# Spreading the rows of 8x8 blocks: two float32r products of 296 columns in place of one fp32 product of 392

## The chip, the cores and the metric

The kernel runs on one core of a Trainium2 chip. The metric is device microseconds of one execution; the number compared is the median of several runs. TensorE is called PE below (PEld is its weight load), VectorE DVE, ScalarE ACT, GpSimd POOL.

## The reference, cut to what matters

One decoder block on 512 tokens of width 1024: a stick-breaking attention branch and an RWKV-7 branch side by side, gated and merged, then an MLP and a gated embedding. The change lies in the RWKV-7 branch, whose recurrence is

```
state = state * w_t + (state a_t) b_t^T + v_t k_t^T
y     = state r_t
```

over 8 heads of 64 by 64. The kernel does it in chunks of 64 tokens. For each chunk and head, it needs the inverse of a unit triangular 64x64 matrix (one plus a strictly triangular matrix made of a and b). That inverse is built from the small blocks up: 8x8 blocks on the diagonal by substitution, then 32x32, then 64x64.

## The kernel before

After the attention (to about 140 us) comes the stage that holds the change, to about 400 us. It has one round for each of the four pairs of heads (pairs 0 to 3 here). A round has three kinds of work, which a scheduler puts in one fixed order on each engine:

- the fill: large products of the projections, `mm3`, three float32r matmuls of 512 columns for each step (L191, L192, L193, into `ps_m`; below "main matmuls"), with a cast of their weights on ACT (L175) and its remainder on DVE (L176), and the evacuations `u` (L304) and `gg` (L678) with `mix` (L306);
- `prepare` of the next pair: it makes the inputs of the recurrence. Two groups of products of `Q` and `BK` (L787) give the matrices, which DVE masks into `LM` (L792) and `DE` (L795). Then the inverse follows: DVE cuts out the 8x8 blocks (`own8`, L828), transposes `LM` in four quarters (L838), and adds the blocks' rows up to `L8` (L831). Then L833 puts `L8` times a selection of rows into `Ls`, a product with a block matrix of ones (L840) spreads every row over the 8 partitions of its block, and seven steps of DVE substitution (L849, L850) read it from PSUM. L851 expands the result into `own8`, and three products `times` (L817) and two more steps (L876, L884) go on to 32 and 64;
- `scan` of the pair before: 8 chunks one after the other, each with a product of the state on PE (L935), a sum on DVE (`UV`, L937), a second product (L944), and two updates of the state on DVE (`S`, L952).

PE and DVE take their instructions in the scheduler's order, so a wait of PE for one of the small results holds the fill behind it. `Ls` lies before the change in a buffer of the pool `tmp`, whose five buffers many other steps share.

The lines of the inverse that the change replaces:

```
Ls = tmp()[:, 0:392].rearrange("p (s k i) -> p s k i", s=7, k=8)
dve.tensor_tensor(out=Ls, in0=L8[..., 1:8] (7 times), in1=s8[..., 0:7], op=ALU.mult)
ps = ps_gen()[:, 0:392]
product_ = pe.matmul(ps, cc(K_BO8, P), Ls, start=True, stop=True)
```

Of the kernel before, what the change touches and what calls it, by code (L numbers as in the profile page):

```python
# [11 lines left out]
F32R = mybir.dt.float32r  # L12
BF16 = mybir.dt.bfloat16
AF = mybir.ActivationFunctionType
ALU = mybir.AluOpType
# [3 lines left out]
P = 128  # L19
# [31 lines left out]
K_ID, K_ONE, K_STRICT, K_INCL, K_B8, K_O8, K_S8, K_BO8, K_BO, K_TRI, K_NEG, K_CAUS = range(12)  # L51
# [34 lines left out]
def tile_block(ctx: ExitStack, tc: tile.TileContext, xT, xt, pT, wts, lora, cols_d, gfin_d, consts_d, out, dbg=None):  # L86
    nc = tc.nc
    act, dve, pool, pe, sync = nc.scalar, nc.vector, nc.gpsimd, nc.tensor, nc.sync
# [3 lines left out]
    def r32(ap):  # L92
        return ap.bitcast(F32)
# [20 lines left out]
    def cc(k, w):  # L114
        return cst[:, COFF[k]:COFF[k] + w]
# [161 lines left out]
    with ExitStack() as sA:  # L277
# [43 lines left out]
        with ExitStack() as s1:  # L321
# [12 lines left out]
            ps = ps_z()  # L334
# [242 lines left out]
        with ExitStack() as s2:  # L577
            p2 = s2.enter_context(tc.tile_pool(name="p2", bufs=1))
# [17 lines left out]
            pool.memset(Z, 0.0)  # L596

            NBIG, NMID = 9, 3

            def ps_gen():  # L600
                return ps2.tile([P, T], F32, name="ps_g", bufs=3)
# [13 lines left out]
            for hp in range(HP):  # L615
                csl = slice(hp * P, (hp + 1) * P)
                for i, (name, got) in enumerate((("w0", cum_), ("a0", a_all))):
                    ps = ps_gen()
                    pe.matmul(ps, lw[:, i, csl], lx[:, i], start=True, stop=False)
                    pe.matmul(ps, lw[:, i, csl], lxl[i], start=False, stop=True)  # L620
                    t = p2.tile([P, T], F32, name=name, bufs=HP)
# [9 lines left out]
            def tmp(dt=F32):  # L631
                return p2.tile([P, T], dt, name="tmp", bufs=5)
# [53 lines left out]
            def prepare(hp, got):  # L686
# [18 lines left out]
                ps = yield from head_sums(sq)  # L705
# [37 lines left out]
                ps = yield from head_sums(ke)  # L743
# [6 lines left out]
                for g in range(2):  # L750
                    ps = ps_gen()
                    for c in range(4):
                        pe.transpose(out=ps[:, c * P:(c + 1) * P],
                                     in_=BK[:, g * 4 + c, :, :].rearrange("p s t -> p (s t)"), identity=ident)
# [3 lines left out]
                ps = ps_gen()  # L758
# [8 lines left out]
                ps = ps_gen()  # L767
# [9 lines left out]
                for g in range(2):  # L777
# [11 lines left out]
                    for hh in range(2):  # L789
# [3 lines left out]
                                          in1=strict.rearrange("p (o u t) -> p o u t", o=1, u=1).broadcast_to([P, 2, 2, C]),  # L793
                                          op=ALU.mult)
                        dve.tensor_tensor(out=DE[:, hh, g * 4:g * 4 + 4, :].rearrange("p (cp q) t -> p cp q t", q=2),  # L795
                                          in0=ps4[:, :, 0::3, :],
                                          in1=incl.rearrange("p (o u t) -> p o u t", o=1, u=1).broadcast_to([P, 2, 2, C]),
                                          op=ALU.mult)
# [8 lines left out]
                s8 = cc(K_S8, 8)  # L807
# [18 lines left out]
                for r, rows in enumerate(QUADS):  # L826
# [2 lines left out]

                L8, Xt = X8[:, 0], X8[:, 1]  # L830
                dve.tensor_reduce(out=L8, in_=own8.rearrange("p k (b i) -> p k i b", b=4), axis=mybir.AxisListType.X, op=ALU.add)  # L831
                Ls = tmp()[:, 0:392].rearrange("p (s k i) -> p s k i", s=7, k=8)
                dve.tensor_tensor(out=Ls, in0=L8.rearrange("p (o k) i -> p o k i", o=1)[:, :, :, 1:8].broadcast_to([P, 7, 8, 7]),  # L833
                                  in1=s8[:, 0:7].rearrange("p (s o u) -> p s o u", o=1, u=1).broadcast_to([P, 7, 8, 7]), op=ALU.mult)
                yield
                dve.tensor_copy(out=Xt, in_=s8.rearrange("p (o i) -> p o i", o=1).broadcast_to([P, 8, 8]))
                for r, rows in enumerate(QUADS):
                    beside = dve.transpose(out=N[rows], in_=LM[rows, :, r // 2, r % 2 * 32:r % 2 * 32 + 32])  # L838
                ps = ps_gen()[:, 0:392]
                product_ = pe.matmul(ps, cc(K_BO8, P), Ls.rearrange("p s k i -> p (s k i)"), start=True, stop=True)  # L840

                tc.add_manual_dep(product_.ins, beside.ins.name,
                                  mybir.DependencyInfo(mybir.DependencyClass.NoSync, mybir.DependencyReason.DATA), reason="order")
                ps = ps.rearrange("p (s k i) -> p s k i", s=7, k=8)
                dve.tensor_tensor(out=N, in0=N, in1=o8.broadcast_to([P, 8, 32]), op=ALU.mult)
                for i in range(7):
                    n = 7 - i
                    t = own8[:, :, 0:n]
                    dve.tensor_tensor(out=t, in0=ps[:, i, :, i:7], in1=Xt[:, :, i:i + 1].broadcast_to([P, 8, n]), op=ALU.mult)  # L849
                    dve.tensor_tensor(out=Xt[:, :, i + 1:8], in0=Xt[:, :, i + 1:8], in1=t, op=ALU.add)  # L850
                dve.tensor_tensor(out=own8.rearrange("p k (b i) -> p k b i", b=4),  # L851
                                  in0=Xt.rearrange("p k (o i) -> p k o i", o=1).broadcast_to([P, 8, 4, 8]),
# [19 lines left out]
                ps = ps_gen()  # L872
# [553 lines left out]
```

## Time and profile before

| what | us |
|---|---|
| median of 3 runs | 869.69 (869.67 to 869.99) |
| the profiled execution | 869.75 |
| its span | 867.7 |
| PE busy in the span | 851.4 |
| DVE busy in the span | 678.1 |

The profile comes from one execution. Its time is 2.05 us over its span, and 0.06 us over the median. The profile writes an fp32 matmul as two records and a float32r one as one. The durations of matmuls overlap, so the time that PE gives to one is read from start to start, not from its duration.

### The profile page before, as it was taken

The page shows a single profiled execution, that of the slowest core. Times are in us where ns is not written, and L with a number is a line of the kernel's source. Part 1 is how long each engine was busy: PE and PEld are TensorE (multiplying, and loading weights), DVE is VectorE, ACT ScalarE, POOL GpSimd, SP SyncE. Part 2 cuts the span into 40 slices and gives each one's busy share as a digit, 9 for nine tenths or more (in the row PEclk, how much of TensorE's full clock was granted, in tenths as well). Part 3 has the DMA queues.
Part 4 walks back from the last instruction along what each step waited for, and adds up shares of the span by engine and source line. Part 5 has one row for each costly group of instructions (what it writes and reads, how often), then busy time and mean ns, then how long its engine had stood idle before and what let it go on. Part 6 is the DMA issues. An engine that isn't in the chain of part 4 may idle for free.

```text
span 867.7 us, 13424 instructions
## 1 busy us (share of the span) xinstructions
PE 851.4 (98%) x5182; PEld 686.8 (79%) x5182; DVE 678.1 (78%) x1228; ACT 448.6 (52%) x703; POOL 80.4 (9%) x138
## 2 busy tenths in 40 slices
PE   8999999999999999999999999999999999999996
PEld 5778787877777777777888888888888888888885
DVE  7899987896979888776754789858985987697767
ACT  6888887744335343534424464344434543453744
POOL 1432431002302111020000000000000000000000
PEclk9999999999999999999999999999999999999999
DMA  7212212221121224437935621531252034300422
GB/s 269 98 49 66 82 62 85 74 97 51 62 87 57 80 73 153 141 116 258 318 121 181 232 73 38 182 120 49 83 184 98 25 127 164 98 1 0 170 73 98
DMA packets 32272, 95.32 MB, mean 110 GB/s; under 512 B 3664, under 2 KB 3664, under 8 KB 32208
## 3 DMA queue, kind: packets, MB, share of 16 engines
q1 hardware_dynamic: 32208, 94.46, 32.6%
q8 instruction: 41, 0.67, 0.3%
q14 instruction: 23, 0.19, 0.1%
HBM read 83.96 MB, written 10.49 MB: 109 GB/s over the span
## 4 chain that ended last, share of the span: by engine, by line
PE 81%; DVE 10%; ACT 4%; issue 1%; DMA 1%; SPq 0%; POOL 0%; POOLq 0%; DVEq 0%; ACTq 0%
PE ps_m L191 13%; PE ps_m L193 13%; PE ps_m L192 13%; PE ps_m L206 9%; PE ps_m L207 9%; PE ps_m L208 9%; DVE w_lo L176 2%; PE ps_g L817 1%; PE ps_o L497 1%; PE ps_g L193 1%; PE ps_c L935 1%; PE ps_s L944 1%; PE ps_g L191 1%; PE ps_g L192 1%; PE ps_g L906 1%
## 5 line engine op out<-in xcount | busy, mean ns | idle before, releaser
L175 ACT CAST w_hi<-w_raw 128x1024 fp32r<-128x1024 f32 x94 | 99.0, 1053 | 170.4 <-PE ps_m L192 110.8
L176 DVE TENSOR_TENSOR w_lo<-w_raw,w_hi 128x1024 fp32r<-128x1024 f32 x94 | 115.1, 1225 | 37.6 <-ACT w_hi L175 37.2
L191 PE MATMUL ps_m<-h_hi,w_hi 128*128 128x512 f32 x320 | 130.6, 410 | 0.9 <-ACT h_hi L353 0.9
L192 PE MATMUL ps_m<-h_lo,w_hi 128*128 128x512 f32 x320 | 128.0, 400 | 0.0
L193 PE MATMUL ps_m<-h_hi,w_lo 128*128 128x512 f32 x320 | 127.5, 399 | 0.0
L191 PE MATMUL ps_m<-hx,w_hi 128*128 128x512 f32 x256 | 99.6, 390 | 0.4 <-ACT hx L1049 0.4
L192 PE MATMUL ps_m<-hx,w_hi 128*128 128x512 f32 x256 | 99.6, 390 | 0.0
L193 PE MATMUL ps_m<-hx,w_lo 128*128 128x512 f32 x256 | 99.5, 389 | 0.0
L191 PEld LDWEIGHTS ps_m<-h_hi,w_hi 128*128 128x128 f32 x320 | 60.7, 190 | 11.4 <-ACT h_hi L353 1.6
L193 PEld LDWEIGHTS ps_m<-h_hi,w_lo 128*128 128x128 f32 x320 | 60.3, 188 | 11.8
L192 PEld LDWEIGHTS ps_m<-h_lo,w_hi 128*128 128x128 f32 x320 | 60.5, 189 | 11.0 <-DVE h_lo L354 1.1
L191 PEld LDWEIGHTS ps_m<-hx,w_hi 128*128 128x128 f32 x256 | 48.0, 188 | 10.5 <-ACT hx L1049 0.6
L192 PEld LDWEIGHTS ps_m<-hx,w_hi 128*128 128x128 f32 x256 | 48.1, 188 | 10.2 <-DVE hx L1050 0.2
L193 PEld LDWEIGHTS ps_m<-hx,w_lo 128*128 128x128 f32 x256 | 48.0, 188 | 10.0
L207 PE MATMUL ps_m<-w_lo,fS 128*128 128x512 f32 x128 | 49.8, 389 | 0.0
L208 PE MATMUL ps_m<-w_hi,fS 128*128 128x512 f32 x128 | 49.8, 389 | 0.0
L206 PE MATMUL ps_m<-w_hi,fS 128*128 128x512 f32 x128 | 49.8, 389 | 0.0
L1291 POOL TENSOR_SCALAR r<-s 128x1 f32<-128x1 f32 x1 | 0.5, 519 | 478.9 <-DVE t L1271 478.9
L208 PE MATMUL ps_m<-w_hi,fA 128*128 128x512 f32 x96 | 37.4, 389 | 0.0
L207 PE MATMUL ps_m<-w_lo,fA 128*128 128x512 f32 x96 | 37.3, 389 | 0.0
L206 PE MATMUL ps_m<-w_hi,fA 128*128 128x512 f32 x96 | 37.3, 389 | 0.0
L221 ACT CAST fS<-sums 128x256 fp32r<-128x256 f32 (+1 forms) x32 | 19.8, 620 | 33.3 <-DVE sums L1141 33.3
(378 smaller groups left out, 1911.6 us busy)
## 6 DMA issues: line engine op xcount, KB each, us to landing
w_raw<-in_wts_dram SPq DMA_DIRECT2D x98, 512.0 KB, 3.5
gates<-gg SPq DMA_DIRECT2D x16, 256.0 KB, 2.1
x_in<-in_xT_dram SPq DMA_DIRECT2D x8, 256.0 KB, 5.7
tmp<-gates SPq DMA_DIRECT2D x8, 256.0 KB, 4.0
upsb<-tmp SPq DMA_DIRECT2D x8, 256.0 KB, 3.5
ga<-upsb SPq DMA_DIRECT2D x8, 256.0 KB, 5.4
gb<-gates SPq DMA_DIRECT2D x8, 256.0 KB, 5.4
xs<-in_xt_dram SPq DMA_DIRECT2D x4, 512.0 KB, 5.9
```

Of the source, the lines that this page charges most:

```text
L175: act.copy(out=hi, in_=raw)
L176: dve.tensor_tensor(out=lo, in0=raw, in1=r32(hi), op=ALU.subtract)
L191: pe.matmul(ps, wh, xh[:, k, t], start=first, stop=False)
L192: pe.matmul(ps, wh, xl[:, k, t], start=False, stop=False)
L193: pe.matmul(ps, wl, xh[:, k, t], start=False, stop=last)
L206: pe.matmul(ps, xh[:, k + j], wh, start=first and j == 0, stop=False, skip_group_check=True)
L207: pe.matmul(ps, xh[:, k + j], wl, start=False, stop=False, skip_group_check=True)
L208: pe.matmul(ps, xl[:, k + j], wh, start=False, stop=last and j == 1, skip_group_check=True)
L221: act.copy(out=hi, in_=src)
L497: pe.matmul(ps_o[:, j * P:T], vv[:, j, hh, :, :].rearrange("p a d -> p (a d)"), part[:, ZB[j]:ZB[j] + ZN[j]], start=j == 2 and part is wh, ...
L817: last = pe.matmul(ps[rows, k], left[rows, k, :], rhs[rows, k], start=True, stop=True)
L906: pe.matmul(ps[:, j * P:(j + 1) * P], Z[:, hh * 4 + g * 2 + cp, :], MA[:, g * 4 + j, :], start=True, stop=True)
```

## The change

`L8` is split by DVE into a float32r part and the remainder, both in a new tile `L8p`. `Ls` becomes a tile of its own with two halves of 296 columns, one for each part. A half leaves out elements that the substitution does not read: rows 0 to 2 keep 7 columns for each of 8 blocks (168 columns), rows 3 to 6 keep 4 (128 columns). Each half is thus made by two DVE multiplications. The product becomes two float32r matmuls, one after the other into the same PSUM tile, with the ones matrix as a float32r copy `bo8` that one more DVE cast makes at the start of the stage. The substitution reads its rows at other places in PSUM; its shapes stay.

```
+            bo8 = p2.tile([P, P], F32R, name="bo8")
+            dve.tensor_copy(out=bo8, in_=cc(K_BO8, P))
+            SPREAD = ((0, 3, 0), (3, 4, 168))
...
-                Ls = tmp()[:, 0:392].rearrange("p (s k i) -> p s k i", s=7, k=8)
-                dve.tensor_tensor(out=Ls, in0=L8.rearrange("p (o k) i -> p o k i", o=1)[:, :, :, 1:8].broadcast_to([P, 7, 8, 7]),
+                L8p = p2.tile([P, 2, 8, 8], F32R, name="L8p")
+                dve.tensor_copy(out=L8p[:, 0], in_=L8)
+                dve.tensor_tensor(out=L8p[:, 1], in0=L8, in1=r32(L8p[:, 0]), op=ALU.subtract)
+                Ls = p2.tile([P, 2, 296], F32R, name="Ls")
+                for u, (s0, n, at) in [(u, x) for u in range(2) for x in SPREAD]:
+                    w = 7 - s0
+                    dve.tensor_tensor(out=Ls[:, u, at:at + n * 8 * w].rearrange("p (s k i) -> p s k i", s=n, k=8),
...
-                ps = ps_gen()[:, 0:392]
-                product_ = pe.matmul(ps, cc(K_BO8, P), Ls.rearrange("p s k i -> p (s k i)"), start=True, stop=True)
+                ps = ps_gen()[:, 0:296]
+                product_ = pe.matmul(ps, bo8, Ls[:, 0], start=True, stop=False)
+                pe.matmul(ps, bo8, Ls[:, 1], start=False, stop=True)
```

The scheduler orders all of the stage anew. On DVE, pair 0, from the sum of the rows (`X` here is the tile of `L8`) to the first evacuation behind the product, the order was:

```order
L831 TENSOR_REDUCE X_1843<-own_1842 128x64
L838 STREAM_TRANSPOSE LX<-LM 32x8x32
L833 TENSOR_TENSOR tmp<-X_1843,cst 128x392
L838 STREAM_TRANSPOSE LX<-LM 32x8x32 x2
L678 TENSOR_TENSOR gg<-ps_m,rs 128x512
```

It is now, in the same place:

```order
L835 TENSOR_REDUCE X_1845<-own_1844 128x64
L850 STREAM_TRANSPOSE LX<-LM 32x8x32
L838 CAST L8p<-X_1845 128x64
L850 STREAM_TRANSPOSE LX<-LM 32x8x32
L839 TENSOR_TENSOR L8p<-X_1845,L8p 128x64
L843 TENSOR_TENSOR Ls<-L8p,cst 128x168
L843 TENSOR_TENSOR Ls<-L8p,cst 128x128
L843 TENSOR_TENSOR Ls<-L8p,cst 128x168
L843 TENSOR_TENSOR Ls<-L8p,cst 128x128
L850 STREAM_TRANSPOSE LX<-LM 32x8x32
L682 TENSOR_TENSOR gg<-ps_m,rs 128x512
```

Six instructions stand where one stood, and one of the two transpositions behind it has moved ahead of them. The rows are the same in the other pairs.

On PE, pair 3, around the product (`ps_s` and `ps_c` are the two products of the scan), the order was:

```order
L192 MATMUL ps_m<-h_lo,w_hi 128x512
L840 MATMUL ps_g<-tmp,cst 128x392
L944 MATMUL ps_s<-UV,BKt 128x128
L193 MATMUL ps_m<-h_hi,w_lo 128x512
L191 MATMUL ps_m<-h_hi,w_hi 128x512
L192 MATMUL ps_m<-h_lo,w_hi 128x512
L193 MATMUL ps_m<-h_hi,w_lo 128x512
L191 MATMUL ps_m<-h_hi,w_hi 128x512
L192 MATMUL ps_m<-h_lo,w_hi 128x512
L193 MATMUL ps_m<-h_hi,w_lo 128x512
L935 MATMUL ps_c<-S_1570,Q 128x128
```

It is now:

```order
L192 MATMUL ps_m<-h_lo,w_hi 128x512
L852 MATMUL ps_g<-Ls,bo_1582 128x296
L853 MATMUL ps_g<-Ls,bo_1582 128x296
L193 MATMUL ps_m<-h_hi,w_lo 128x512
L958 MATMUL ps_s<-UV,BKt 128x128
L191 MATMUL ps_m<-h_hi,w_hi 128x512
L192 MATMUL ps_m<-h_lo,w_hi 128x512
L193 MATMUL ps_m<-h_hi,w_lo 128x512
L949 MATMUL ps_c<-S_1570,Q 128x128
L191 MATMUL ps_m<-h_hi,w_hi 128x512
L192 MATMUL ps_m<-h_lo,w_hi 128x512
L958 MATMUL ps_s<-UV,BKt 128x128
```

The scan's steps stand closer together behind the product: 1, 3 and 2 main matmuls lie between them in place of 0, 7 and 6.

The main matmuls between the last L787 and the product number 23, 24, 21 and 20 in pairs 0 to 3 before, and 25, 24, 26 and 24 after. In pairs 1 and 3 the new order has among them the two scan steps that pair 2 had before (`ps_s`, 9 main matmuls, `ps_c`); in pair 2 it has the one that pair 1 had (`ps_c`, then all main matmuls). The two matmuls of the product have a wait each, the first for the first half of `Ls`, the second for the second. Between the product and the first `times` there are 25, 38, 35 and 43 main matmuls before, and 38, 40, 38 and 40 after.

## Rows read from the trace of the kernel before

**Rows 1.** The page: busy time of the engines, and the chain that ended last by engine.

```profile
PE 851.4 (98%) x5182; PEld 686.8 (79%) x5182; DVE 678.1 (78%) x1228; ACT 448.6 (52%) x703; POOL 80.4 (9%) x138
...
PE 81%; DVE 10%; ACT 4%; issue 1%; DMA 1%; SPq 0%; POOL 0%; POOLq 0%; DVEq 0%; ACTq 0%
```

**Rows 2.** Busy time by stretch: the stretch, its length, then PE, PEld, DVE, ACT and POOL busy with counts, the granted clock of PE, DMA share and GB/s.

```profile
260.00:300.00 40.00, 39.44 (x353) 30.35 (x351) 35.42 (x87) 16.97 (x26) 8.45 (x14) 1.00 0.22 73
```

**Rows 3.** The timeline of PE around the product of pair 0: start, duration, engine, instruction, and in brackets the idle time before it and what ended it.

```profile
186.38 0.39 PE L193 MATMUL ps_m<-h_hi,w_lo 128*128 128x512 f32 x1
...
186.60 0.39 PE L191 MATMUL ps_m<-h_hi,w_hi 128*128 128x512 f32 x1
...
187.12 0.30 PEld L840 LDWEIGHTS ps_g<-tmp,cst 128*128 128x128 f32 x2 [0.55 <-DVE tmp L833]
187.12 0.93 PE L840 MATMUL ps_g<-tmp,cst 128*128 128x392 f32 x2
...
187.58 0.69 PE L192 MATMUL ps_m<-h_lo,w_hi 128*128 128x512 f32 x1
...
188.11 0.39 PE L193 MATMUL ps_m<-h_hi,w_lo 128*128 128x512 f32 x1
```

**Rows 4.** The same for pairs 1, 2 and 3: the main matmul ahead of the product, and the product.

```profile
233.49 0.39 PE L192 MATMUL ps_m<-h_lo,w_hi 128*128 128x512 f32 x1
...
234.44 0.93 PE L840 MATMUL ps_g<-tmp,cst 128*128 128x392 f32 x2 [0.56 <-DVE tmp L833]
...
286.10 0.39 PE L192 MATMUL ps_m<-h_lo,w_hi 128*128 128x512 f32 x1
...
286.66 0.93 PE L840 MATMUL ps_g<-tmp,cst 128*128 128x392 f32 x2 [0.17 <-DVE tmp L833]
...
337.42 0.39 PE L192 MATMUL ps_m<-h_lo,w_hi 128*128 128x512 f32 x1
...
337.78 0.93 PE L840 MATMUL ps_g<-tmp,cst 128*128 128x392 f32 x2
```

**Rows 5.** The timeline of PE in the attention: float32r matmuls of 256 and of 384 columns that follow each other.

```profile
81.22 0.28 PE L497 MATMUL ps_o<-wh,vv 128*128 128x256 f32 x1
81.33 0.28 PE L497 MATMUL ps_o<-wl,vv 128*128 128x256 f32 x1
...
81.92 0.33 PE L509 MATMUL ps_z<-sums_hi,neg 128*128 128x384 f32 x1
82.09 0.34 PE L509 MATMUL ps_z<-sums_lo,neg 128*128 128x384 f32 x1
```

**Rows 6.** The timeline of DVE ahead of the product of pair 0.

```profile
182.69 0.41 DVE L792 TENSOR_TENSOR LM<-ps_g,cst 128x256 f32<-128x256 f32 x1
...
183.02 0.41 DVE L795 TENSOR_TENSOR DE<-ps_g,cst 128x256 f32<-128x256 f32 x1
...
185.44 0.56 DVE L831 TENSOR_REDUCE X<-own 128x64 f32<-128x256 f32 x1
...
186.03 0.43 DVE L838 STREAM_TRANSPOSE LX<-LM 32x256 f32<-32x256 f32 x1
...
186.50 0.57 DVE L833 TENSOR_TENSOR tmp<-X,cst 128x392 f32<-128x392 f32 x1
...
187.10 0.89 DVE L838 STREAM_TRANSPOSE LX<-LM 32x256 f32<-32x256 f32 x2
```

**Rows 7.** Groups of DVE instructions by line and shape: count, busy us and mean ns of one, and the idle time before them with what ended it.

```profile
L536 DVE CAST bones<-first 128x128 fp32r<-128x128 f32 x1 | 0.2, 219 | 0.0
...
L836 DVE COPY X<-cst 128x64 f32<-128x64 f32 x4 | 0.7, 163 | 3.1 <-DMA o_sb<-oo 3.1
...
L478 DVE TENSOR_TENSOR sums<-sp,sums 128x128 f32<-128x128 f32 x8 | 2.4, 294 | 0.0
...
L849 DVE TENSOR_TENSOR own<-ps_g,X 128x56 f32<-128x56 f32 x4 | 0.8, 203 | 0.0
```

**Rows 8.** The timeline of pair 2, between its two groups of L787: the second group on PE, and `UV` and the first mask of the second group on DVE.

```profile
279.89 1.13 PE L787 MATMUL ps_g<-Q,BK 64*128 64x128 f32 x14
...
280.43 0.29 DVE L937 TENSOR_TENSOR UV<-ps_c,UV 64x128 f32<-64x128 f32 x1
280.86 0.42 DVE L792 TENSOR_TENSOR LM<-ps_g,cst 128x256 f32<-128x256 f32 x1
```

**Rows 9.** The waits of PE in the stage: PE instruction, what it waited for, us in total, times, longest.

```profile
PE ps_s L944 <- DVE UV L937: 0.9, 3, 0.3
```

**Rows 10.** The timeline of PE at `times`: the first product of pair 0, the first of pair 3, the third of pair 3, and L884 in pair 0.

```profile
194.19 0.74 PE L817 MATMUL ps_g<-LX,own 32*32 32x32 f32 x64 [0.45 <-DVE own L851]
...
203.52 0.58 PEld L884 LDWEIGHTS ps_g<-Z,LX 32*32 32x32 f32 x32 [0.37 <-issue]
...
350.13 0.64 PEld L817 LDWEIGHTS ps_g<-LX,own 32*32 32x32 f32 x64 [0.47 <-DVE own L851]
...
355.08 0.64 PEld L817 LDWEIGHTS ps_g<-LX,LB 32*32 32x32 f32 x64 [1.15 <-DVE LX L863]
```

**Rows 11.** The timeline of DVE in pair 1: from the start of an evacuation, over a weight's remainder and the end of a mix with two steps of the substitution between them, to the start of L851.

```profile
242.44 0.67 DVE L304 TENSOR_TENSOR u<-ps_m,rs 128x512 f32<-128x512 f32 x1
...
244.99 0.41 DVE L851 TENSOR_TENSOR own<-X,cst 128x256 f32<-128x256 f32 x1
```

More of the change, by code (lines that the diff above doesn't have):

```diff
@@ L831, in prepare @@
                 dve.tensor_reduce(out=L8, in_=own8.rearrange("p k (b i) -> p k i b", b=4), axis=mybir.AxisListType.X, op=ALU.add)
-                Ls = tmp()[:, 0:392].rearrange("p (s k i) -> p s k i", s=7, k=8)
-                dve.tensor_tensor(out=Ls, in0=L8.rearrange("p (o k) i -> p o k i", o=1)[:, :, :, 1:8].broadcast_to([P, 7, 8, 7]),
-                                  in1=s8[:, 0:7].rearrange("p (s o u) -> p s o u", o=1, u=1).broadcast_to([P, 7, 8, 7]), op=ALU.mult)
+                L8p = p2.tile([P, 2, 8, 8], F32R, name="L8p")
[5 more added lines that the diff above has]
+                    dve.tensor_tensor(out=Ls[:, u, at:at + n * 8 * w].rearrange("p (s k i) -> p s k i", s=n, k=8),
+                                      in0=r32(L8p[:, u:u + 1, :, 1 + s0:8]).broadcast_to([P, n, 8, w]),
+                                      in1=s8[:, s0:s0 + n].rearrange("p (s o u) -> p s o u", o=1, u=1).broadcast_to([P, n, 8, w]),
+                                      op=ALU.mult)
                 yield
@@ L838, in prepare @@
                     beside = dve.transpose(out=N[rows], in_=LM[rows, :, r // 2, r % 2 * 32:r % 2 * 32 + 32])
-                ps = ps_gen()[:, 0:392]
-                product_ = pe.matmul(ps, cc(K_BO8, P), Ls.rearrange("p s k i -> p (s k i)"), start=True, stop=True)
+                ps = ps_gen()[:, 0:296]
+                product_ = pe.matmul(ps, bo8, Ls[:, 0], start=True, stop=False)
+                pe.matmul(ps, bo8, Ls[:, 1], start=False, stop=True)
                 tc.add_manual_dep(product_.ins, beside.ins.name,
                                   mybir.DependencyInfo(mybir.DependencyClass.NoSync, mybir.DependencyReason.DATA), reason="order")
-                ps = ps.rearrange("p (s k i) -> p s k i", s=7, k=8)
+                rows_ = [ps[:, at:at + n * 8 * (7 - s0)].rearrange("p (s k i) -> p s k i", s=n, k=8)[:, j, :, j:7 - s0]
+                         for s0, n, at in SPREAD for j in range(n)]
                 dve.tensor_tensor(out=N, in0=N, in1=o8.broadcast_to([P, 8, 32]), op=ALU.mult)
@@ L848, in prepare @@
                     t = own8[:, :, 0:n]
-                    dve.tensor_tensor(out=t, in0=ps[:, i, :, i:7], in1=Xt[:, :, i:i + 1].broadcast_to([P, 8, n]), op=ALU.mult)
+                    dve.tensor_tensor(out=t, in0=rows_[i], in1=Xt[:, :, i:i + 1].broadcast_to([P, 8, n]), op=ALU.mult)
                     dve.tensor_tensor(out=Xt[:, :, i + 1:8], in0=Xt[:, :, i + 1:8], in1=t, op=ALU.add)
```

## Prediction

> **What bounds the kernel now.** I read the page first. PE is busy for 851.4 of 867.7 us and carries 81% of the chain that ended last; DVE carries 10% of it [rows 1]. Then I read the busy time by stretch: in the rounds of the stage PE is busy for 39.44 of 40 us at the full granted clock, and DVE for 35.42 [rows 2]. So PE is the bound, and what it does is worth its full price; but DVE is close behind it, and each result of DVE that comes late holds the whole queue of PE. Last I read the timelines of both engines around the product, where the change lies. A main matmul takes 0.23 us from start to start. Ahead of the product of pair 0, PE could have gone on at 186.60 + 0.23 = 186.83, and the product starts at 187.12, when `Ls` is there: a wait of 0.29 us [rows 3]. By the same reading pairs 1, 2 and 3 wait for 0.72, 0.33 and 0.13 us [rows 4]. PE already waits for `Ls` in all four pairs, 1.47 us in sum. That decides how the change is to be costed: whatever DVE takes longer for `Ls` goes to the path, unless the new order of PE has more work ahead of the product.
>
> **The product itself.** From its start at 187.12 to where the next main matmul would have started by the pace of those behind it (188.11 - 0.23 = 187.88), the fp32 product takes 0.76 us of PE [rows 3]. Float32r matmuls that follow each other take 0.11 us for 256 columns and 0.17 us for 384 [rows 5], so 296 take 0.13, and two take 0.27 (bounds 0.22 and 0.34). PE gains 0.49 us for each pair, **1.96 us** in all (1.7 to 2.2).
>
> **When Ls is ready.** Before, the second transposition starts at 186.03, L833 at 186.50, and `Ls` is there at 187.07 [rows 6]. Now, from 186.50: the cast of 64 elements (0.16, as the copy of 64), a transposition (0.43 and 0.04 of change-over on either side), the remainder (0.20, as the 56 elements of L849), then the four multiplications [rows 6, 7]. A multiplication of 128 elements takes 0.29, one of 168 lies between that and 0.41 for 256; I take 0.33 [rows 6, 7]. DVE instructions that don't need each other start 0.08 before the end of the one ahead: 0.41 long, 0.33 from start to start [rows 6]. That gives the cast to 186.66, the transposition to 187.12, the remainder to 187.36, the first half of `Ls` to 187.83 and the second to 188.29. The first half is **0.76 us later**, the second **1.22**. At full length plus 0.03 of change-over each it would be 0.97 and 1.65. One transposition (0.44) less stands behind them.
>
> **What PE does meanwhile.** Pair 0 has 2 main matmuls more ahead of the product: the wait for the first half is 0.29 + 0.76 - 0.46 = 0.59. The second matmul then waits for 1.22 - 0.76 - 0.13 = 0.33 in every pair: 0.92 in sum. Pair 2 now has the order of pair 1 before, with 2 more: 0.72 + 0.76 - 0.46 + 0.33 = 1.35. Pairs 1 and 3 have that of pair 2 before, with 3 more: 0.33 + 0.76 - 0.69 + 0.33 = 0.73. In pair 1 DVE has besides the remainder of a head sum (0.60) between the two groups of masks, and PE reaches the second group 2 main matmuls (0.46) sooner. DVE was only 0.14 early there, from the end of `UV` at 280.72 to 280.86 [rows 8], so 0.60 + 0.46 - 0.14, about 0.9, come on top: 1.63. Pair 3 has one main matmul less there, 0.1: 0.83. The four waits make 0.92 + 1.63 + 1.35 + 0.83 = 4.73 us, against 1.47 now: **+3.26 us**. So the product's own gain is more than taken back at its own place.
>
> **What stands behind it.** L944 now waits for `UV` three times, 0.31 each [rows 9], since the two transpositions stand ahead of `UV`. With one transposition behind `Ls`, and 2, 2 and 1 main matmuls between, I get 0.15, 0.15 and 0.37: **-0.3**. At the first `times`, pair 0 now waits 0.45 for `own8` [rows 10]. DVE gets an evacuation, a weight's remainder and a mix ahead of it (2.55 us less 0.15 for the small steps between, so 2.4 [rows 11]) and loses 0.44; PE gets 13 main matmuls (2.96) and loses 0.63 of the product. The wait goes: **-0.4**. In pair 3 PE has 3 main matmuls less (0.69) and 0.63 less of the product, DVE 0.44 less: a wait of 0.12 (0.47 less the 0.35 or so that stands ahead of such products with no wait at all, as at L884 [rows 10]) becomes 1.0: **+0.9**, in part already at the scan's steps, which stand closer there. The third `times` of pair 3 waits 1.15 - 0.35 = 0.8 [rows 10] and gets 2 main matmuls more ahead of it: **-0.45**. Pairs 1 and 2 come out even. The cast of `bo8` (0.22 [rows 7]) stands where the copy into `X` now waits 3.1 us for a store [rows 7]; it takes over that wait, and the evacuation behind it on DVE is only 0.1 later. I cost it at nothing, since PE has its fill there; it costs 0.2 if that cover is gone. `Ls` leaves the pool `tmp`, which could end a wait of a later `tmp`: 0 to -0.3, taken as nothing.
>
> **The sum.** -1.96 + 3.26 - 0.3 - 0.4 + 0.9 - 0.45 = +1.05 us on the profiled 869.75, which lies 0.06 over the median: **870.7 us**, no change that a measurement of this kernel can tell, for it tells about 0.2% or 1.74 us (867.95 to 871.43). The terms that I read from other pairs in place of the pair itself (the waits of pairs 1 to 3, and those at `times`) are each good to some 0.5 us; together that is about 1.2 us either way.
>
> **The rivals.** *The waits do not grow* (faster). The scheduler has moved main matmuls ahead of the product in pairs 0, 2 and 3 and the first `times` of pair 0 further back. If DVE reaches the masks earlier than in the pairs that I took as patterns, by 0.7 us or more in each pair, the waits stay at their 1.5 us and only the product's gain is left: 869.7 - 1.96 = 867.7. For it speaks that DVE is not full (35.42 of 40), against it that all four pairs wait now. It decides for faster from 2.8 us less wait than I have. *The short DVE instructions do not overlap* (slower). The second half of `Ls` and the remainder hang on results of just before, and the row that shows 0.33 from start to start is of instructions that do not. At full length plus 0.03 of change-over, the second half comes after 1.65 and not 1.22, 0.43 later in each pair, 1.7 us in all: 872.4. The point from which it makes the kernel measurably slower is 0.7 us, that is 0.18 in each pair, or 0.30 from one multiplication to the next and not 0.25. [...] *The product is not cheaper* (slower): if the float32r product took what the fp32 one takes, the time would be 870.7 + 1.96 = 872.7. The rows of the attention speak against it [rows 5].
>
> **How the numbers follow.** My forecast, within 0.2%, gets 0.53. The waits that do not grow, faster by over 0.2%, get 0.15. Slower by over 0.2% gets 0.32: 0.27 for the short instructions (with the errors of the patterns to that side), 0.05 for the product. The range goes from 867.8 to 872.8. Below it I leave out about half of the first rival, above it half of the last and the far part of the second, in sum 0.18.
>
> **What would show it.** Two matmuls of L852 and L853 with 0.13 us of PE each, and ahead of each a wait for `Ls`, 0.4 to 1.3 us for the first and about 0.3 for the second. DVE rows of 0.16, 0.20, 0.33 and 0.29 us, with 0.25 from one multiplication to the next. A PE busy time some 2 us down with the span up, or level. A first `times` with no wait in pair 0, and one of about 1 us in pair 3. The prediction is wrong if the first matmul finds its half ready, or if PE's waits in the stage outside these places change by more than 1 us, for the whole stage was ordered anew and I followed only the places around the product.

## The result, and the profile after

| | median us | runs | lowest to highest |
|---|---|---|---|
| before | 869.43 | 12 | 868.60 to 870.18 |
| after | 871.83 | 12 | 870.59 to 877.53 |

The changed kernel takes 1.0041 times as long (95% interval 1.0024 to 1.0057): 2.4 us more, slower by more than the 0.2% that a measurement can tell. The profiled execution of it took 871.73 us, 1.98 more than that of the kernel before.

The page of the changed kernel, busy times and the chain that ended last:

```profile
PE 851.4 (98%) x5182; PEld 686.1 (79%) x5182; DVE 682.3 (78%) x1249; ACT 448.8 (52%) x703; POOL 76.8 (9%) x138
...
PE 77%; DVE 13%; ACT 4%; DMA 3%; issue 2%; SPq 0%; POOL 0%; POOLq 0%; DVEq 0%; ACTq 0%
```

PE is as busy as before, DVE 4.2 us more, and DVE's share of the chain has gone from 10 to 13%, DMA's from 1 to 3 [rows 1].

The timeline of PE at the product of pair 0 (start, duration, engine, instruction, idle time before it), against [rows 3]:

```profile
186.62 0.39 PE L193 MATMUL ps_m<-h_hi,w_lo 128*128 128x512 f32 x1
187.48 0.40 PE L852 MATMUL ps_g<-Ls,bo 128*128 128x296 f32 x1 [0.47 <-DVE Ls L843]
187.93 0.40 PE L853 MATMUL ps_g<-Ls,bo 128*128 128x296 f32 x1
188.16 0.40 PE L191 MATMUL ps_m<-h_hi,w_hi 128*128 128x512 f32 x1
```

The first half waits for `Ls`; the second starts 0.45 after it, and the next main matmul 0.23 after that. On DVE, the same place, against [rows 6]:

```profile
185.60 0.43 DVE L850 STREAM_TRANSPOSE LX<-LM 32x256 f32<-32x256 f32 x1
186.06 0.19 DVE L838 CAST L8p<-X 128x64 fp32r<-128x64 f32 x1
186.29 0.43 DVE L850 STREAM_TRANSPOSE LX<-LM 32x256 f32<-32x256 f32 x1
186.75 0.23 DVE L839 TENSOR_TENSOR L8p<-X,L8p 128x64 fp32r<-128x64 f32 x1
186.90 0.97 DVE L843 TENSOR_TENSOR Ls<-L8p,cst 128x168 fp32r<-128x168 f32 x4
```

The four multiplications overlap: 0.97 us from the start of the first to the end of the last. The waits of PE's matmuls in the stage (instruction, what it waited for, us in total, times, longest):

```profile
PE ps_g L852 <- DVE Ls L843: 2.2, 4, 0.7
PE ps_g L821 <- DVE LX L877: 1.8, 2, 1.5
PE ps_c L1001 <- DVE y L996: 0.6, 1, 0.6
```

The wait of 1.5 is at the third `times` of pair 3. The timelines of ACT, DVE and PE there:

```profile
356.34 0.63 ACT L671 ACTIVATE tmp<-tmp 128x512 f32<-128x512 f32 x1 [2.22 <-DMA tmp<-gates]
358.91 0.63 ACT L671 ACTIVATE tmp<-tmp 128x512 f32<-128x512 f32 x1 [1.95 <-DMA tmp<-gates]
359.45 0.56 ACT L980 COPY y<-ps_c 64x512 f32<-64x512 f32 x1
```

```profile
357.12 0.45 DVE L827 STREAM_TRANSPOSE LB<-LX 128x256 f32<-128x256 f32 x1
360.64 0.69 DVE L989 TENSOR_REDUCE st<-y 128x8 f32<-128x512 f32 x1 [3.08 <-ACT y L980]
361.24 0.44 DVE L827 STREAM_TRANSPOSE LB<-ps_g 128x256 f32<-128x256 f32 x1
361.61 0.39 DVE L877 TENSOR_TENSOR LX<-ps_g,LX 128x256 f32<-128x256 f32 x1
```

```profile
362.05 0.75 PE L821 MATMUL ps_g<-LX,LB 32*32 32x32 f32 x64 [1.52 <-DVE LX L877]
```

A gate's load lands late, ACT's sigmoid waits for it, the copy of the scan's `y` stands behind the sigmoid, DVE's reduction of `y` stands ahead of the transposition and L877, and PE waits for these.

To compare kernels place by place I add up PE's rows: for each instruction the time from the end of the work ahead of it to its own end, its waits included, and then by place. Two numbers in one row differ by what a place costs PE. For the profiled executions (us):

| place | before | after |
|---|---|---|
| the product (four pairs) | 4.53 | 5.57 |
| the scan's steps, L944 and L935 before | 18.78 | 18.95 |
| `times` | 11.66 | 11.48 |
| transpositions of `y` at the end of a scan | 2.04 | 2.58 |
| the sums of squares of the first norm | 0.91 | 1.62 |

The last row is at 20 us, ahead of everything that the change touches; a second trace of the changed kernel has 1.21, and the other kernels 0.9 (but for e2, 1.25). So 0.71 of this trace's 1.98 us are not the change's. The other places, taken together, come out 0.3 lower after.

### The profile page after: what moved, and what is told of

Its sections match the earlier page's. It is cut to its first block, busy times and chain, and to the rows that moved or that the text cites. A ratio compares the mean times of both kernels' runs of the same rounds, so it can differ in the third digit from the quotient of the medians.

```text
span 869.7 us, 13447 instructions
## 1 busy us (share of the span) xinstructions
PE 851.4 (98%) x5182; PEld 686.1 (79%) x5182; DVE 682.3 (78%) x1249; ACT 448.8 (52%) x703; POOL 76.8 (9%) x138
## 4 chain that ended last, share of the span: by engine, by line
PE 77%; DVE 13%; ACT 4%; DMA 3%; issue 2%; SPq 0%; POOL 0%; POOLq 0%; DVEq 0%; ACTq 0%
PE ps_m L191 13%; PE ps_m L192 13%; PE ps_m L193 12%; PE ps_m L208 9%; PE ps_m L207 9%; PE ps_m L206 9%; DVE w_lo L176 2%; DMA w_raw<-in_wts_dram 1%; DMA tmp<-gates 1%; PE ps_g L821 1%; PE ps_o L497 1%; PE ps_g L920 1%; PE ps_z L505 1%; PE ps_g L791 1%; DVE own L832 1%
```

## The experiments

Two theories stood at first. *A*: DVE's longer way to `Ls` is the price. *B*: the new order, which the scheduler made of the whole stage, costs half or more, above all through the third `times` of pair 3 and the last scan. Medians below are set against the runs of the kernel before on the same chip.

**e1 and e2: `y` ahead of the gates.**

```
-                        with tc.issue_after(state["norm"].ins):
-                            act.activation(out=ga, in_=ga, func=AF.Sigmoid)
...  (behind the matmuls of the step:)
+                        with tc.issue_after(state["norm"].ins), (tc.issue_after(state["y"].ins) if "y" in state else nullcontext()):
+                            act.activation(out=ga, in_=ga, func=AF.Sigmoid)
...
```

> The changed kernel with one edit: ScalarE's sigmoids of the loaded gates are queued behind its copies of the scan's y in pair 3, so that no y copy stands behind a wait for a gate's transfer. Nothing is left out. Theory A (about half of the loss is made at the product, where PE waits for Ls, and about 0.8 us more at the third times of pair 3, where DVE stands behind ScalarE's y copies): PE's idle time ahead of the third times of pair 3 falls from 1.52 to 0.7 us or less, and the time from 871.8 to about 871.0. Theory B (all of the loss is at the product; the wait at the third times only moves): that wait falls, but the time stays at 871.8 within 0.4. Theory C (DVE is the bound there, with or without ACT): the wait stays at 1.3 to 1.6 us, and the time at 871.8.

> The same edit in the kernel before, as a control. Nothing is left out. There the y copies stood behind the gates' sigmoids too, but these waited less long. Theory A: the wait ahead of the third times of pair 3 is 0.71 us and falls by 0.4 at most; the time stays within 0.4 us of the 869.4 of the kernel before, so that the edit gives the changed kernel at least 0.4 us more than this one. If this one gains as much as the changed one, the y copies don't explain a difference between the two.

e1: 873.18 us (1.0035, 1.0023 to 1.0047). The wait at the third `times` fell from 1.52 to 0.27, with 0.49 more a moment later that nothing in the profile ends; and a new one came at the end of the last scan:

```profile
PE ps_c L1003 <- ACT gb L1101: 0.8, 1, 0.8
```

e2: 869.88 (1.0000, 0.9992 to 1.0009). The edit gains nothing in either kernel, and e1's time lies above what any of the three theories gave. That wait is not what the changed kernel loses.

**e3 and e4: the two halves of the change, each alone.** e3 keeps the split and drops the packing; e4 keeps the packing and drops the split.

```
e3:
-            SPREAD = ((0, 3, 0), (3, 4, 168))
+            SPREAD = ((0, 7, 0),)
-                Ls = p2.tile([P, 2, 296], F32R, name="Ls")
+                Ls = p2.tile([P, 2, 392], F32R, name="Ls")
...
e4:
...
-                product_ = pe.matmul(ps, bo8, Ls[:, 0], start=True, stop=False)
-                pe.matmul(ps, bo8, Ls[:, 1], start=False, stop=True)
+                product_ = pe.matmul(ps, cc(K_BO8, P), Ls, start=True, stop=True)
```

> The changed kernel without the packing: two float32r parts of 392 columns, each made by one multiplication in place of two. Nothing is left out; the order of instructions on the engines is that of the changed kernel. Theory A (the two parts' way through DVE holds PE): a multiplication of 392 elements takes 0.57 us, two about 1.06 from start to end against 0.97 for the four, and each matmul 0.17 against 0.13; the first half is there some 0.04 us later and the second 0.1, so 4 x 0.18 = 0.7 us more: 872.2 to 872.8. Rival (what costs is the number of short instructions on DVE, 24 more in all): with 8 fewer of them it is faster than the changed kernel by 0.5 us or more, 871.3 or below.

> The kernel before with the packing alone: an fp32 product of 296 columns, made by two multiplications on DVE (168 and 128 elements). Nothing is left out. Theory A (the split is what costs): the product takes 0.76 x 296/392 = 0.57 us of PE in place of 0.76, and DVE is no later (0.24 + 0.29 = 0.53 against 0.57 us), so 4 x 0.19 = 0.76 us less: 868.5 to 869.2. Rival (the packed layout, or any change of the order around pair 3, costs as much as in the changed kernel): 870.5 or more.

e3: 872.06 (1.0034, 1.0020 to 1.0047), level with the changed kernel: without the packing the loss stays. The measurement can't tell the 0.7 us that theory A adds. e4: 870.43 (1.0004, 0.9996 to 1.0013), where theory A had 868.5 to 869.2. The product did fall, from 4.53 to 3.79, but the transpositions of `y` rose from 2.04 to 2.98: in the scheduler's new order the gain went at the last scan.

**e5: the first part alone, in the scheduler's order.**

```
-                dve.tensor_tensor(out=L8p[:, 1], in0=L8, in1=r32(L8p[:, 0]), op=ALU.subtract)
...
-                for u, (s0, n, at) in [(u, x) for u in range(2) for x in SPREAD]:
+                for u, (s0, n, at) in [(u, x) for u in range(1) for x in SPREAD]:
...
-                pe.matmul(ps, bo8, Ls[:, 1], start=False, stop=True)
```

> The changed kernel with the first of the two parts alone: the cast, two multiplications and one matmul. It leaves out the remainder of L8, its two multiplications and the second matmul. Theory A (what the second part costs at the product is what the change loses): PE's time at the product falls from 5.57 us by the four second matmuls with their waits, 4 x 0.45 = 1.8, and DVE has 12 instructions less; the time goes to 869.8 to 870.4, level with the kernel before or faster. Theory B (the order around pair 3 and the last scan, which the scheduler also changes, costs as much): the product falls to 3.8 us, but the time stays above 870.8, and the transpositions of the last scan's y still wait 0.5 us or more.

e5: 871.76 (1.0019, 1.0007 to 1.0030). Both theories missed the product: it stays at 5.26, with longer waits for the one half (1.2 the longest), since the scheduler's order is another: 23, 21, 20 and 25 main matmuls stand ahead of it, in place of the changed kernel's 25, 24, 26 and 24. A change of DVE's work and a change of order can't be told apart this way; the later runs hold the order.

**e6: the mask in the weights.**

```
+            for s_ in range(7):
+                pool.tensor_scalar(out=bo7[:, s_, :], in0=cc(K_BO8, P), scalar1=cc(K_S8, 8)[:, s_:s_ + 1], scalar2=None, op0=ALU.mult)
...
+                    mm = pe.matmul(ps7[:, s_, :, s_:7], bo7[:, s_, :], L8[:, :, 1 + s_:8], start=True, stop=True)
```

> The kernel before with no multiplication for Ls at all: the mask is put into the weights once (seven matrices of 128x128, made by GpSimd at the start of the stage), and the product is seven fp32 matmuls of 8 x 7 down to 8 x 1 columns, 224 in all, straight from L8. Nothing is left out. Theory A (PE waits for DVE there, so DVE's time on the way is the price): the multiplication of 0.57 us is gone from the way, and the waits of 1.5 us in sum fall to 0.3; by the fp32 product's 1.94 ns for a column 224 columns take 0.43 us, with seven starts an estimated 0.5 to 0.9; sum between -2.2 and -0.6 us: 867.3 to 869.4. Rival (seven short matmuls with a weight load each cost 0.2 us apiece or more, 1.4 us for each pair): 870.8 or more.

e6: 878.03. PE takes 6.31 us for the four products, 1.58 each against 1.13 of the kernel before with its waits, so the rival is right. The total says less, for GpSimd made the masks ahead of a tile that PE needs, and PE stood for 3.99 us at 151.89; that is my kernel's doing.

**e7 and e8: the gates' loads.**

```
-                        sync.dma_start(out=ga, in_=gates[:, i * 2 + m, :])
+                        pool.dma_start(out=ga, in_=gates[:, i * 2 + m, :])
```

> The changed kernel with the loads of the gates issued by GpSimd in place of SyncE, where they stand behind stores that wait for DVE. Nothing is left out; the order on PE, DVE and ACT stays up to the third times of pair 3. Theory C (late gates, which ACT's sigmoids wait for, hold y and then PE in pair 3, now more and now less from one execution to the next, and make the long tail of the changed kernel's times): ACT's waits for tmp from gates fall from 11.2 us to under 5, no time lies above 873, and the median goes to 871.0 or below. Rival (they only move PE's wait to the last scan, as the kernel with y ahead showed): 871.5 to 872.5 with PE waiting 0.8 us or more at the transpositions of the last y.

> The changed kernel again, for a second trace of it. Theory C: the wait at the third times of pair 3 differs from the 1.52 us of the first trace by 0.5 us or more, with the landing of the gates; the waits at the product stay within 0.1 us of 0.47, 0.68, 0.74 and 0.28. If the time lies above 873, the trace shows where.

e7: 880.07 (1.0107, 1.0089 to 1.0125), far above both expectations. The loads land later, not sooner: ACT waits 14.2 us for gates, against 11.2, and PE 2.12 us at the third `times` of pair 3 and 4.23 at the last `y`, and behind the two the granted clock was 0.70 from 363 to 366 us and 0.50 from 410.5 to 413. It shows how far PE hangs on these loads, but not what the change costs. e8, the unchanged source: 871.34. Its waits in the stage:

```profile
PE ps_g L852 <- DVE Ls L843: 2.2, 4, 0.7
PE ps_c L1001 <- DVE y L996: 1.0, 1, 1.0
PE ps_g L821 <- DVE LX L877: 0.5, 2, 0.3
```

The 1.52 us at the third `times` are 0.27 here, and the last scan's wait is 0.95 in place of 0.64. The product's waits are the same to 0.04. ACT waits 7.5 us for gates, in place of 11.2. So the wait at `times` differs from one execution to the next with the landing of a gate, and the total hardly does.

**e9 and e10: arithmetic and order crossed.** A table holds, for every engine, in which order the scheduler of one kernel had put its instructions; order edges along it, which wait for nothing, force it upon the other kernel.

```
+        for a, b in zip(chain, chain[1:]):
+            tc.add_manual_dep(b, a.name, mybir.DependencyInfo(mybir.DependencyClass.NoSync, mybir.DependencyReason.DATA), reason="order")
...
```

> The changed kernel's arithmetic, with every engine's instructions held in the order of the kernel before, by order edges from a table; what the change adds stands where the multiplication for Ls and the product stood. Nothing is left out. Both theories: PE's time at the product is 5.2 to 5.8 us, since first halves come 0.38 us later than before's Ls (0.19 + 0.23 + 0.53 - 0.57) and second halves 0.31 after them. Theory A (the loss is that, and DVE's longer way, whatever the order): 870.5 to 872.0, and times above 873 as with the changed kernel. Theory B (half of the loss or more is the new order, through the third times of pair 3 and the last scan): those waits are back at 0.7 and 0.1 us, the time is 869.8 to 870.4, and no time lies above 872.

> The reverse: the arithmetic of the kernel before (one multiplication, one fp32 product of 392 columns), with the order of the changed kernel on every engine. Ls has a buffer of its own, as in the changed kernel. Nothing is left out. Theory A: PE's time at the product is 3.1 to 4.2 us, since 2 to 6 main matmuls more stand ahead of it, and the time is that of the kernel before or less, 868.5 to 869.6. Theory B: PE waits 0.5 us or more at the transpositions of the last y and up to 1.5 at the third times of pair 3, as in the changed kernel; 870.4 to 871.5, with some times above 872.5.

| | order of before | order of after |
|---|---|---|
| arithmetic of before | 869.43 (the kernel before) | 869.47, 1.0001 (0.9988 to 1.0014) |
| arithmetic of after | 875.53, 1.0062 (1.0048 to 1.0076) | 871.83, 1.0041 (1.0024 to 1.0057) |

Theory B is refuted: the new order alone costs nothing that shows, and the new arithmetic costs 5.6 us in the old order. The scheduler's new order had taken back more than half of that. Theory A was not right in size either. e9's product took the 5.57 us that both had, but its time lies above A's range: the scan's steps took 20.44 in place of 18.78, `times` 12.69 in place of 11.66, and the granted clock fell to 0.50 for 3.0 us (last section), an estimated 1.5 us lost, half of the 3.0; all six executions of e9 have a mean granted clock of 0.993 to 0.995. e10's time is in A's range, but its product (4.51) is not. The waits of e10, in the changed order, where L840 is the product and L833 the multiplication:

```profile
PE ps_g L817 <- DVE LX L863: 1.0, 2, 0.7
PE ps_c L987 <- DVE y L982: 0.9, 1, 0.9
PE ps_g L840 <- DVE Ls L833: 0.7, 2, 0.4
```

The wait at the last `y` does come with the order, as B said, but the order saves as much elsewhere: the scan's steps take 17.72 in place of 18.78 and `times` 10.72 in place of 11.66.

**e11 and e12: the product later.** In the order of before, only PE's table is changed: each product stands three main matmuls later.

> The packing alone (fp32, 296 columns, two multiplications), in the order of the kernel before on every engine but for one thing: each of the four products stands three main matmuls later on PE. Nothing is left out. Theory A and B: PE no longer waits for Ls (0.69 us of matmuls cover waits of 0.1 to 0.7), so the four products take 4 x 0.57 = 2.3 in place of 4.5 us, and DVE is not later: 867.2 to 867.9. Rival (DVE's chain behind the product decides, so that a product 0.7 us later makes the first times 0.7 later, too): 869.0 or more, with longer waits at times.

> The changed kernel's arithmetic in the order of the kernel before, with each product (both halves) three main matmuls later on PE. Nothing is left out. If PE's waits are the whole price, the products take 4 x 0.27 = 1.1 us and residual waits of up to 1: 866.3 to 867.5. If DVE's longer way (0.7 us for each pair) shows behind it, at times, up to 2.6 us come back: 867.5 to 869.5.

e11: 873.55 (1.0039, 1.0025 to 1.0053). e12: 878.01 (1.0093, 1.0079 to 1.0107). Both expectations failed. The product fell as hoped, to 2.00 and 1.71 us. But in pairs 1 to 3 the scan's L944 stands directly behind the product. With the product behind the next three main matmuls, PE comes to L944 sooner by the product's time and its wait, and waits there for `UV`, which DVE makes behind `Ls`: 1.71, 1.32 and 1.16 us in e11, 2.53, 2.15 and 1.96 in e12. The scan's steps took 24.20 and 26.42 us, and e12's granted clock fell to 0.50 from 345.5 to 348.7 us besides. Here, taking a wait of PE away by moving PE's work only moved the wait.

**e13 to e16: DVE's work and `Ls`'s place, in the order of the changed kernel.** e13 is e5 with that order held. e14 to e16 move the multiplications for `Ls` (in e14 with the cast and the remainder) directly behind the reduction to `L8`; the two transpositions that stood between come behind them.

```
DVE, order of the changed kernel:              e14:
  reduction to L8                                reduction to L8
  transposition                                  cast, remainder
  cast                                           four multiplications for Ls
  transposition                                  transposition
  remainder, four multiplications for Ls         transposition
  transposition                                  transposition
```

> The first part alone again (it leaves out the remainder of L8, its two multiplications and the second matmul), but with every engine's instructions held in the order of the changed kernel; with the scheduler's own order it had gained nothing. Theory A (DVE's time on the way to Ls and behind it is the price): per pair DVE has 0.2 + 0.5 us less, PE no second matmul with its wait, 4 x 0.45 = 1.8, and a first half 0.2 us earlier, 0.8 in all; 868.3 to 869.4. Rival (PE's waits there come from the order and stay, whatever DVE does): 870.5 or more, with 5 us or more at the product.

> The changed kernel, all of its arithmetic and its order, but for one thing on DVE: the cast, the remainder and the four multiplications stand directly behind the reduction to L8, and the two transpositions that stood between them stand behind them. DVE does the same work in the same time. Theory A1 (the delay of Ls at the product is what costs): the first half comes 0.85 us earlier, the first waits (3.2 us in sum) fall to 0.5 or less, the seconds stay at 0.31 each; PE's time at the product 2.4 to 3.1, and the time 868.4 to 869.6. Theory A2 (DVE's work as such is what costs, since what stands behind Ls, UV and times, is as late as before): the product falls as much, the waits for UV and at times grow or stay, 870.3 or more.

> The packing alone (fp32, 296 columns, two multiplications) in the order of the changed kernel, with the two multiplications directly behind the reduction. Nothing is left out. Theory A1: no wait for Ls, four products of 0.57, 2.3 us in place of 4.5 of the kernel before in that order; 866.9 to 867.8, below both kernels. Theory A2: the product falls, but not the time below 868.6.

> The arithmetic of the kernel before in the order of the changed kernel, with the multiplication directly behind the reduction, as a control for both. Nothing is left out. Theory A1: the waits for Ls go (1.5 us), products of 0.76 stay: PE's time there 3.0 to 3.3, the time 867.8 to 868.6. Theory A2: 869.0 to 869.8, as in that order with the multiplication behind the transpositions.

All of these stand in the order of the changed kernel; DVE's busy time is the page's, the times of the product and of the scan's steps are added up as above, and the last column is the median less that of the kernel before beside it. The ratio is that of the means, in which long executions weigh more:

| kernel | DVE busy | product | scan's steps | median | ratio | less before |
|---|---|---|---|---|---|---|
| after | 682.3 | 5.57 | 18.95 | 871.83 | 1.0041 (1.0024 to 1.0057) | +2.40 |
| e14, after, `Ls` first | 682.4 | 1.99 | 21.54 | 871.59 | 1.0021 (1.0013 to 1.0030) | +1.66 |
| e13, first part alone | 680.0 | 3.22 | 18.82 | 869.49 | 0.9998 (0.9990 to 1.0007) | -0.44 |
| e10, arithmetic of before | 679.2 | 4.51 | 17.72 | 869.47 | 1.0001 (0.9988 to 1.0014) | -0.44 |
| e16, before, `Ls` first | 679.5 | 2.63 | 18.69 | 868.69 | 0.9992 (0.9981 to 1.0002) | -1.24 |
| e15, packing alone, `Ls` first | 679.3 | 1.99 | 19.01 | 868.27 | 0.9978 (0.9968 to 0.9987) | -1.66 |

The time goes with DVE's work, and far less with PE's time at the product. e14 against the changed kernel takes 3.6 us off the product and 0.7 off the time. e14 against e16: the product is 0.6 us cheaper, DVE has 2.9 us more, and the time is 2.9 us longer. The changed kernel against e10: DVE 3.1 us more, the time 2.8 longer. Product and scan's steps together go with the time: 24.52 in the changed kernel and 23.53 in e14, but 22.23 in e10, 22.04 in e13, 21.32 in e16 and 21.00 in e15. For the changed arithmetic theory A2 holds. e15 and e16 lie between A1's times and A2's: without the split, 1.9 us less at the product (e10 to e16) came with 0.8 us less time, and the two intervals overlap. e13 missed theory A's range by 0.1, and its rival by 1.0. Where PE stands in e14 instead:

```profile
PE ps_s L961 <- DVE UV L954: 2.6, 3, 1.0
PE ps_c L1004 <- DVE y L999: 1.5, 1, 1.5
```

Its DVE and PE in pair 1 show how:

```profile
235.30 0.97 DVE L844 TENSOR_TENSOR Ls<-L8p,cst 128x168 fp32r<-128x168 f32 x4
236.31 1.34 DVE L853 STREAM_TRANSPOSE LX<-LM 32x256 f32<-32x256 f32 x3
237.68 0.28 DVE L954 TENSOR_TENSOR UV<-ps_c,UV 64x128 f32<-64x128 f32 x1
```

```profile
236.57 0.40 PE L192 MATMUL ps_m<-h_lo,w_hi 128*128 128x512 f32 x1
236.80 0.39 PE L193 MATMUL ps_m<-h_hi,w_lo 128*128 128x512 f32 x1
238.01 0.49 PE L961 MATMUL ps_s<-UV,BKt 128*128 128x128 f32 x2 [0.82 <-DVE UV L954]
```

DVE goes from `Ls` over the transpositions to `UV` without a gap; `UV` is as late as DVE's sum of work makes it, wherever `Ls` stands.

e15 is faster than both kernels: 1.7 us below the one before, its interval wholly below 1. It has three things at once: the order of the changed kernel, `Ls` first, and the packing, which costs DVE nothing. e16 has the first two and is 1.24 below; the 0.4 us that would be the packing's own share are not clear of the two intervals, and the packing alone in the scheduler's order (e4) gained nothing.

## Why the prediction was wrong

- **What bounds the kernel now** was the step that failed, and with it the term for `UV` behind the product. I took PE as the bound, "and what it does is worth its full price", gave DVE room from a mean over 40 us [rows 2], and followed its longer way only to the product. Here is the kernel before from the masks to the first `times` in pairs 0 to 3 (stretch, length, then as in [rows 2]):

```profile
179.00:197.40 18.40, 17.82 (x146) 13.71 (x144) 17.78 (x46) 5.53 (x7) 0.00 (x0) 1.00 0.28 90
229.50:245.90 16.40, 15.52 (x84) 11.52 (x86) 15.74 (x47) 3.35 (x4) 2.16 (x3) 1.00 0.29 92
281.00:297.40 16.40, 15.92 (x101) 12.04 (x103) 15.81 (x48) 3.87 (x5) 3.04 (x5) 1.00 0.27 90
332.70:350.50 17.80, 17.44 (x119) 13.35 (x119) 17.00 (x46) 6.12 (x7) 2.17 (x3) 1.00 0.45 142
```

  DVE is idle there for 0.6 to 0.8 us in each pair; of the 4.6 idle us in the 40 of [rows 2], 4.0 lie outside the stretch of pair 2. PE is as full there, and which of the two decides is told by the runs in one order. DVE could not take 0.7 us more in each pair (3.1 less 0.2 for `bo8`, by 4) unnoticed: in the same order the change gave PE less work and DVE 3.1 us more, and the time followed DVE: 2.8 us.
- **The product itself**: predicted -1.96, two matmuls of 0.13. In e13, where one half is all, the product starts at 188.02 and the next main matmul at 188.26: 0.24, so two take 0.47 and the gain is 4 x (0.76 - 0.47) = 1.2. Each matmul was taken too small by 0.1; [rows 5] were no pattern for it.
- **When `Ls` is ready**: right. The cast took 0.19 (0.16), the remainder 0.23 (0.20), the four multiplications 0.97 from the first start to the last end, as the overlap of 0.08 gives (three starts of 0.25 or so and one end of 0.29: 1.0). From the start of the transposition ahead, `Ls` was there at 1.03 us before, and its halves at 1.83 and 2.27 now: 0.80 and 1.24 later, where 0.76 and 1.22 had been worked out. The rival of short instructions without overlap gave 872.4, near the measured time, but for a cause that the rows refute: a multiplication of 168 or 128 elements lasts 0.28 to 0.33, but the next one starts after 0.20 to 0.24.
- **What PE does meanwhile**: predicted a product place 1.30 us dearer (-1.96 + 3.26), measured 1.04 (4.53 to 5.57). Two errors cancel: dearer matmuls, shorter waits. First halves waited 0.63, 0.84, 0.90 and 0.44 us (from the start of the main matmul ahead, less 0.23), where 0.59, 1.30, 1.02 and 0.50 had been worked out; the starts of the two halves lie 0.45 apart, where 0.46 had been.
- **What stands behind it**: -0.3 for `UV` was the mis-sized term. Against the arithmetic of before in the same order (e10), the scan's steps cost 1.23 and 1.25 more in the two traces of the changed kernel (18.95 and 18.97 to 17.72), next to 1.06 and 1.12 at the product, about 2.3 in sum; in e13, with one half alone, the sum is 0.2 less than in e10. I had counted behind the product only what the new order brings; but `UV` stands behind the same work of DVE, and comes later by it. For `times` (+0.05) the traces disagree: 11.48 and 10.25 against 10.72 in e10, with the landing of a gate, so that DVE's longer way costs something there is not shown. Of single terms, the first `times` of pair 0 lost its wait (-0.4, right), that of pair 3 did not get the 0.9, and the third of pair 3 was 0.81 longer in one trace and 0.44 shorter in the other (-0.45 predicted).
- **Not followed at all**: the last scan. Its `y` waits 0.64 to 0.95 in the changed kernel and hardly at all before. I had named it as a sign of being wrong, since the rest of the stage was ordered anew; its transpositions took 0.54 us more in the first trace and 0.85 in the second. This comes with the order: e10, level with the kernel before, waits 0.89 there.
- **The sum** of +1.05 is near what the two traces show outside the first norm against the trace of before, 1.27 and 1.29, but that is luck, for its terms are others: the product's place +1.04 and +1.09 (predicted +1.30), the scan's steps +0.17 and +0.19 (-0.3), `times` -0.18 and -1.41 (+0.05), the last `y` +0.54 and +0.85 (nothing). The rest of the 2.4 us between the medians is not placed by a trace: the traced execution of before lies 0.32 over its median, that of the changed kernel 0.10 under its own.
- **The rival that the waits do not grow** is refuted by e9 and by the rows; *the product is not cheaper* by the 0.24 of e13, for two take 0.47 and not 0.76.

What stays open: why executions of the changed kernel spread up to 877.53. The three longest have a lower mean granted clock (0.995 to 0.996 against 0.997 to 0.999), and the last section shows one way to that, but none of them was profiled. Such executions are not the new arithmetic's alone: e10 goes up to 873.76, at 0.995.

## What to carry to other kernels

Before an edit that trades work of one engine for work of another, take the stretch where it stands and ask which engine's work, made longer, is late at the next three places that wait for it, not only at the first. To learn whether arithmetic or order makes a difference under a scheduler, hold the order and change the arithmetic, and the reverse: the cross of e9 and e10 settled what the partial edits could not. A wait that goes when work is moved, while the total hardly follows, was where the cost showed and not what made it. And a mean busy time over a long window does not tell whether an engine has room: read it over the stretch in which the work has to be done.

## What the runs showed of the hardware

*A wait of PE cost twice.* In e16 PE stood for 2.06 us ahead of the last `y` (in a long execution, 871.25 against a median of 868.69). The busy time by stretch (stretch, length, PE busy, granted clock, DMA share, GB/s):

```profile
398.20:400.30 2.10, 0.09 (x1) 1.00 0.79 247
400.30:403.50 3.20, 3.15 (x8) 0.51 0.80 284
403.50:407.00 3.50, 3.50 (x17) 0.96 0.02 5
```

Behind the wait the granted clock was 0.51 for 3.2 us, and float32r matmuls of 512 columns went 0.42 us from start to start in place of 0.23:

```profile
403.33 0.62 PE L191 MATMUL ps_g<-osb,w_hi 128*128 128x512 f32 x1
403.75 0.43 PE L192 MATMUL ps_g<-osb,w_hi 128*128 128x512 f32 x1
...
404.25 0.39 PE L191 MATMUL ps_g<-osb,w_hi 128*128 128x512 f32 x1
404.48 0.40 PE L192 MATMUL ps_g<-osb,w_hi 128*128 128x512 f32 x1
```

Behind the 1.52 us in the changed kernel's trace it stayed at 1.00. In e9 it fell to 0.50 from 290.5 to 293.5, behind waits of 0.50 and 0.83 us close together. So in these runs the length of one wait does not tell. In e12 PE stood for 2.53, 2.15 and 1.96 us for `UV` in pairs 1 to 3, and the clock fell only behind the last and shortest (the stretches right behind the three waits):

```profile
238.00:241.50 3.50, 2.79 (x15) 1.00 0.00 0
292.00:295.50 3.50, 2.98 (x15) 1.00 0.10 40
345.50:348.70 3.20, 3.20 (x11) 0.50 0.50 156
```

In e16 the clock was back at 0.96 in the stretch behind 3.15 us of work. What sets it was not tried.

*A short float32r matmul was not short.* The one of 296 columns took 0.24 us from its start to the next (the second half, in all four pairs of the changed kernel's trace), as much as a main matmul of 512 (0.23), while [rows 5] show 0.11 for 256 and 0.17 for 384. The weight loads show where the time lies: that of the main matmul behind starts 0.11 after the second half's own, and the matmul 0.13 after its load; in the attention the load for the matmul at 81.33 starts with the one ahead, at 81.22 [rows 5].

```profile
187.92 0.19 PEld L853 LDWEIGHTS ps_g<-Ls,bo 128*128 128x128 f32 x1 [0.26 <-DVE Ls L843]
188.03 0.19 PEld L191 LDWEIGHTS ps_m<-h_hi,w_hi 128*128 128x128 f32 x1
```

```profile
81.22 0.19 PEld L497 LDWEIGHTS ps_o<-wl,vv 128*128 128x128 f32 x1
```

In e14, where the first half of pair 0 waits for nothing, the second starts 0.19 after it. What makes the load start late was not tried.
